# Sharing single columns between two paths, TensorE with ScalarE and VectorE, at the end of a masked reconstruction loss

## The chip, the cores and the metric

One core of a Trainium2 chip. The metric is device time in microseconds (us) of one execution. Beside it every run lists its *span*, from the first to the last recorded instruction of the program, and its mean TensorE clock. The kernel before takes 77.2 us, so 1% is 0.77 us.

## The reference, cut to what matters

```python
batch, num_patches, dim = 32, 196, 768        # 147 patches of each batch row are masked
mean = target.mean(axis=-1, keepdims=True)
var = target.var(axis=-1, keepdims=True)
target = (target - mean) / np.sqrt(var + 1e-6)
loss = np.mean((pred - target) ** 2, axis=-1)
return loss.mean(axis=-1)                      # 32 numbers
```

Two inputs of 4704 x 768 float32, 28.9 MB in all, are read once; 128 bytes are written.

## The kernel before

A batch row's 147 patches lie on four partitions, 37 on three of them and 36 on the fourth. A "column" is patch c of every partition, a tile of 128 x 768. Each column is loaded (all but the first targets cast to bfloat16 on the way), VectorE takes its statistics, ScalarE the root, VectorE the reciprocal, and GpSimd writes the normalised target `s`. Then (pred - s) is squared and summed by one of three ways:

```python
units = [((c, c + 1), 0, D, "ACT" if c < 18 else "DVE+ACT") for c in range(0, 24, 2)]
units.insert(2, ((REST,), 0, D, "ACT"))
units += [((24,), 0, D, "DVE"), ((25,), 0, D, "DVE+ACT"), ((26, 27), 0, D, "DVE+ACT")]
units += [((c,), 0, D, "ACT" if c % 2 else "DVE") for c in range(28, KM - 1)]
units += [((KM - 1,), 0, half, "ACT"), ((KM - 1,), half, D, "ACT")]
# ...
# "ACT": PE adds -s and pred in PSUM through identity matrices, ScalarE squares and sums
# "DVE+ACT": VectorE takes the difference, ScalarE squares and sums
# "DVE": VectorE does both
def difference(u, d0, w):
    z = zs[u, d0] = diffs.tile([P, 2 * D], BF16, name="zd")              # 4 buffers
    # ...
    pin(nc.vector.tensor_tensor(out=z[:, :w], in0=til[:, o:o + w], in1=s[:, so + d0:so + d0 + w],
                                op=ALU.subtract))

def square_dve(u, d0, w, dest):
    z = zs[u, d0][:, :w]
    pin(nc.vector.scalar_tensor_tensor(out=z, in0=z, scalar=1.0, in1=z, op0=ALU.mult, op1=ALU.mult,
                                       accum_out=dest))
```

KM is 36, so column 35 is the last; its pred is loaded in two halves of 384. The order of instructions on each engine is fixed when the kernel is built, by a list scheduler in the kernel that works with estimated durations and with earliest times for what has to land first. At the end small matmuls with a mask add the partial sums over partitions into `acc`; VectorE copies it and one transfer writes it.

Of the kernel before, what the change touches and what calls it, by code (L numbers as in the profile page):

```python
# [7 lines left out]
F32 = mybir.dt.float32  # L8
BF16 = mybir.dt.bfloat16
ALU = mybir.AluOpType  # L10
ACTF = mybir.ActivationFunctionType
# [3 lines left out]
def kernel(  # L15
# [7 lines left out]
    nc = tc.nc  # L23
    pin = tc.keep_in_program_order
    B, N, D = pred.shape
    eps = 1e-6
    P = 128
    J = P // B
    KJ = (N + J - 1) // J
    KM = N - (J - 1) * KJ  # L30
    assert KJ == KM + 1
    RP = B * (J - 1)
    half = D // 2
    BANK = 512
    REST = KM
# [4 lines left out]
    def rows_of(c):  # L40
        return RP if c == REST else P
# [3 lines left out]
    diffs = ctx.enter_context(tc.tile_pool(name="diffs", bufs=4))  # L45
    small = ctx.enter_context(tc.tile_pool(name="small", bufs=8))
    singles = ctx.enter_context(tc.tile_pool(name="singles", bufs=1))
    psum = ctx.enter_context(tc.tile_pool(name="psum", bufs=2, space=bass.MemoryType.PSUM))
    psum1 = ctx.enter_context(tc.tile_pool(name="psum1", bufs=1, space=bass.MemoryType.PSUM))


# [30 lines left out]
    groups += [(c, c + 1) for c in range(16, KM, 2)]  # L82


    units = [((c, c + 1), 0, D, "ACT" if c < 18 else "DVE+ACT") for c in range(0, 24, 2)]
    units.insert(2, ((REST,), 0, D, "ACT"))
    units += [((24,), 0, D, "DVE"), ((25,), 0, D, "DVE+ACT"), ((26, 27), 0, D, "DVE+ACT")]
    units += [((c,), 0, D, "ACT" if c % 2 else "DVE") for c in range(28, KM - 1)]
    units += [((KM - 1,), 0, half, "ACT"), ((KM - 1,), half, D, "ACT")]



# [3 lines left out]
    def op(name, engine, dur, needs, fn, rank=0.0, early=0.0):  # L96
        by_name[name] = len(ops)
        ops.append((name, engine, dur, needs, fn, rank, early))
# [13 lines left out]
            KIND[kind].setdefault(c, []).append((d0, d1, til, (c - c0) * w))  # L112


    land, lanes, clock = {}, {"hw": [], "hw2": [], "sw": []}, 2.9
    for i, (kind, c0, c1, d0, d1, q) in enumerate(stream):
        w = (c1 - c0) * (d1 - d0)
        clock += w * rows_of(c0) / P * 0.915 / D + (0.0 if w >= 4 * D else 0.04)
        lanes[q].append(clock + 1.1)
        for c in range(c0, c1):  # L120
            land[kind, c, d0] = clock + 1.1
        k = len(lanes[q])
        op(("load", i), {"hw": "SP", "hw2": "ACT", "sw": "POOL"}[q], 0.6, [], lambda a=stream[i]: load(*a), rank=-1.0,
           early=0.0 if k <= 8 else lanes[q][k - 9] + 0.3)

    def landed(kind, c):
        return max(t for (k, cc, d), t in land.items() if k == kind and cc == c)

    ident = singles.tile([P, P], BF16)
# [25 lines left out]
    def bn(out, parts):  # L155

        n = parts[0].shape[0]
        st = small.tile([P, len(parts), 6], F32, name="st")
        for j, x in enumerate(parts):
            pin(nc.vector.bn_stats(out=st[:n, j, :], in_=x))  # L160
        pin(nc.vector.bn_aggr(out=out, in_=st[:n, :len(parts)]))  # L161

    def stats(g, i):
        n, K = rows_of(g[0]), len(g)
        if i == 0:
            mvs[g] = small.tile([P, K, 2], F32, name="mv")
        if not norm_pix_loss:
            return
        (_, _, til, o), = tbuf[g[i]]
        bn(mvs[g][:n, i], [til[:n, o + a:o + a + half] for a in (0, half)])  # L170

    def root(g):
        n, K = rows_of(g[0]), len(g)
        r = small.tile([P, K], F32, name="r")
        nm = small.tile([P, K], F32, name="nm")
        for i, c in enumerate(g):
            rs[c] = (r[:n, i:i + 1], nm[:n, i:i + 1])
        rs[g] = r
        if not norm_pix_loss:
            pin(nc.vector.memset(r, 1.0))  # L180
            pin(nc.vector.memset(nm, 0.0))
            return
        mv = mvs[g]
        pin(nc.scalar.activation(out=r[:n], in_=mv[:n, :, 1], func=ACTF.Sqrt, bias=eps_t[:n], scale=1.0))  # L184
        pin(nc.scalar.activation(out=nm[:n], in_=mv[:n, :, 0], func=ACTF.Copy, scale=-1.0))  # L185

    def recip(g):
        n = rows_of(g[0])
        if norm_pix_loss:
            pin(nc.vector.reciprocal(out=rs[g][:n], in_=rs[g][:n]))  # L190

    for k, g in enumerate(groups):
        for i, c in enumerate(g):
            op(("bn", c), "DVE", 1.26, [], lambda g=g, i=i: stats(g, i), rank=k - 50.0, early=landed("t", c))
        op(("root", k), "ACT", 0.55, [("bn", c) for c in g], lambda g=g: root(g), rank=-1.0)
        op(("recip", k), "DVE", 0.2, [("root", k)], lambda g=g: recip(g), rank=-60.0)

# [16 lines left out]
    zs = {}  # L214
# [5 lines left out]
    def product(u, d0, w, src, so, eye, first):  # L220
        n, z = rows_of(u[0]), zs[u, d0]
        for a in range(0, w, BANK):
            b = min(w, a + BANK)
            pin(nc.tensor.matmul(z[:n, a:b], eye[:n, :n], src[:n, so + a:so + b], start=first, stop=not first))  # L224

    def sub_target(u, d0, w):
        if (u, d0) == units[-1][:2]:
            zs[u, d0] = psum1.tile([P, BANK], F32, name="z_last")
        else:
            zs[u, d0] = psum.tile([P, 3 * BANK], F32, name="z")  # L230
        s, so = sbuf[u[0]]
        product(u, d0, w, s, so + d0, nident, True)

# [15 lines left out]
    def square_dve(u, d0, w, dest):  # L249
        z = zs[u, d0][:, :w]  # L250
        pin(nc.vector.scalar_tensor_tensor(out=z, in0=z, scalar=1.0, in1=z, op0=ALU.mult, op1=ALU.mult,  # L251
                                           accum_out=dest))

    tail = 5
    n_early = len(units) - 1 - tail
    rl = singles.tile([P, n_early], F32)
    rl_sum = singles.tile([P, 1], F32)
    finals = []
    early_ops, users, seen = [], [], set()
    for k, (u, d0, d1, eng) in enumerate(units):  # L260
        w = len(u) * D if len(u) > 1 else d1 - d0
        arrive = max(t for (kk, c, d), t in land.items() if kk == "p" and c in u and d < d1)
        norms = [("norm", c) for c in u]
        for c in u:
            if c not in seen:
                op(("norm", c), "POOL", 1.02, [("recip", group_of[c])], lambda u=u, c=c: normalise(u, c), rank=k)
                seen.add(c)
        if k < len(units) - tail:
            if u[0] == REST:
                dest = singles.tile([P, 1], F32, name="rl_rest")  # L270
                finals.append((("sq", k), dest, mask_rest, RP))
            else:
                dest = rl[:, len(early_ops):len(early_ops) + 1]
                early_ops.append(("sq", k))
        else:
            dest = singles.tile([P, 1], F32, name=f"rl{k}")
            finals.append((("sq", k), dest, mask, P))
        if eng in ("DVE", "DVE+ACT"):
            op(("diff", k), "DVE", 0.57 * w / D + 0.05, norms, lambda u=u, d0=d0, w=w: difference(u, d0, w), rank=-2.0,
               early=arrive)  # L280
            if eng == "DVE":
                op(("sq", k), "DVE", 1.0 * w / D, [("diff", k)],
                   lambda u=u, d0=d0, w=w, dest=dest: square_dve(u, d0, w, dest), rank=-1.0)
            else:
                op(("sq", k), "ACT", 0.75 * w / D + 0.25, [("diff", k)],
                   lambda u=u, d0=d0, w=w, dest=dest: square_act(u, d0, w, dest), rank=k)
            continue
        op(("subt", k), "PE", 0.37 * w / D, norms + (users[-2:-1] if k < len(units) - 1 else []) + ["ident"],
           lambda u=u, d0=d0, w=w: sub_target(u, d0, w), rank=k + 0.0)
        op(("pred", k), "PE", 0.37 * w / D, [("subt", k)], lambda u=u, d0=d0, w=w: add_pred(u, d0, w), rank=k,  # L290
           early=arrive)
        op(("sq", k), "ACT", 0.73 * w / D + 0.23, [("pred", k)],
           lambda u=u, d0=d0, w=w, dest=dest: square_act(u, d0, w, dest), rank=k)
        users.append(("sq", k))

    acc = psum1.tile([1, B], F32)
    def early_sum():
        junk = singles.tile([P, n_early], F32, name="junk")
        pin(nc.scalar.activation(out=junk, in_=rl, func=ACTF.Copy, accum_out=rl_sum))

    op("rl_sum", "ACT", 0.4, early_ops, early_sum, rank=50.0)
    finals.insert(0, ("rl_sum", rl_sum, mask, P))
    turn = []

    def final(vec, m, n):
        turn.append(n)
        pin(nc.tensor.matmul(acc, vec[:n], m[:n], start=len(turn) == 1, stop=len(turn) == len(finals)))  # L307

    for i, (need, vec, m, n) in enumerate(finals):
        op(("final", i), "PE", 0.2, [need, "masks"], lambda v=vec, m=m, n=n: final(v, m, n), rank=90.0)  # L310


    HOP = 0.15
# [3 lines left out]
    while left:  # L317
        best = None
        for i in left:
            name, engine, dur, needs, fn, rank, early = ops[i]  # L320
            if any(x not in end for x in needs):
                continue
            t = max([free[engine], early] + [end[x] + (0.0 if ops[by_name[x]][1] == engine else HOP) for x in needs])
# [4 lines left out]
        _, i, t = best  # L328
        name, engine, dur, needs, fn, rank, early = ops[i]
# [43 lines left out]
```

## Time and profile before

| | kernel before |
|---|---|
| time, median of six runs | 77.22 us (77.09 to 77.56) |
| span of the profiled run (its time) | 75.4 us (77.09 us) |
| VectorE busy, instructions | 56.3 us, 148 |
| GpSimd busy | 54.4 us |
| ScalarE busy | 32.0 us |
| last half of column 35: last data record, completion | 71.20 us, 71.50 us |

No engine is busy for more than 75% of the span, but the transfers are busy from the third of forty slices to the thirty-seventh. So a change to engines can only gain at the end, after the stream. The prediction shows the lines of that end. In the profiled run 77.09 - 75.40 = 1.7 us of the time lie outside the span.

### The profile page before, as it was taken

The page shows a single profiled execution, that of the slowest core. Times are in us where ns is not written, and L with a number is a line of the kernel's source. Part 1 is how long each engine was busy: PE and PEld are TensorE (multiplying, and loading weights), DVE is VectorE, ACT ScalarE, POOL GpSimd, SP SyncE. Part 2 cuts the span into 40 slices and gives each one's busy share as a digit, 9 for nine tenths or more (in the row PEclk, how much of TensorE's full clock was granted, in tenths as well). Part 3 has the DMA queues.
Part 4 walks back from the last instruction along what each step waited for, and adds up shares of the span by engine and source line. Part 5 has one row for each costly group of instructions (what it writes and reads, how often), then busy time and mean ns, then how long its engine had stood idle before and what let it go on. Part 6 is the DMA issues. An engine that isn't in the chain of part 4 may idle for free.

```text
span 75.4 us, 570 instructions
## 1 busy us (share of the span) xinstructions
PE 30.3 (40%) x87; PEld 8.7 (11%) x88; DVE 56.3 (75%) x148; ACT 32.0 (42%) x73; POOL 54.4 (72%) x77
## 2 busy tenths in 40 slices
PE   0000000038596540688700778287544000348860
PEld 0000000001232110211100211031111000112220
DVE  0000099999999999976999928960999989989940
ACT  1400000210229802289210297239366099799550
POOL 4998205099999999499989898999878799800000
PEclk9999999999999997555555557965995555555555
DMA  0899999999999999999999999999999999999700
GB/s 0 215 424 339 262 192 236 218 209 215 212 215 215 212 216 225 212 209 215 215 212 215 219 212 225 209 212 202 214 215 209 215 210 210 214 205 205 117 0 0
DMA packets 3973, 15.41 MB, mean 204 GB/s; under 512 B 450, under 2 KB 1186, under 8 KB 3842
## 3 DMA queue, kind: packets, MB, share of 16 engines
q0 software_dynamic: 3712, 13.52, 89.2%
q1 hardware_dynamic: 146, 1.57, 5.7%
q10 hardware_dynamic: 112, 0.29, 1.0%
q14 instruction: 3, 0.02, 0.1%
HBM read 28.90 MB, written 0.00 MB: 383 GB/s over the span
## 4 chain that ended last, share of the span: by engine, by line
DMA 60%; DVE 18%; POOL 9%; issue 6%; PE 2%; ACT 1%; POOLq 0%; ACTq 0%
DMA t<-in_target_dram 49%; DVE st L160 14%; DMA p<-in_pred_dram 11%; POOL s L210 8%; DVE mv L161 3%; DVE zd L246 1%; PE acc L307 1%; POOL t L110 1%; PE z L224 1%; ACT z_last L239 1%; PE z_last L224 1%; POOLq L368 0%; DVE r L190 0%; POOL p L110 0%; DVE ob L336 0%
## 5 line engine op out<-in xcount | busy, mean ns | idle before, releaser
L160 DVE BATCH_NORM_STATS2 st<-t 128x6 f32<-128x384 bf16 (+2 forms) x74 | 36.3, 532 | 11.6 <-DMA t<-in_target_dram 11.6
L210 POOL TENSOR_SCALAR s<-t,nm,r 128x768 bf16<-128x768 bf16 (+2 forms) x37 | 38.2, 1040 | 3.2 <-ACT nm L185 2.0
L224 PE MATMUL z<-s,nident 128*128 128x512 bf16 (+4 forms) x36 | 14.6, 511 | 23.3 <-POOL s L210 17.6
L239 ACT ACTIVATE z<-z 128x1536 f32<-128x1536 f32 (+3 forms) x14 | 16.6, 1184 | 6.9 <-PE z L224 6.8
L224 PE MATMUL z<-p,ident 128*128 128x512 bf16 (+4 forms) x35 | 14.2, 542 | 12.1 <-DMA p<-in_pred_dram 12.0
L184 ACT ACTIVATE r<-mv,eps_t 128x2 f32<-128x2 f32 (+2 forms) x15 | 4.4, 293 | 29.5 <-DVE mv L161 28.8
L110 POOL DMA_DIRECT2D p<-in_pred_dram x18 | 10.2, 565 | 2.7 <-DVE st L160 1.0
L246 DVE TENSOR_TENSOR zd<-p,s 128x768 bf16<-128x768 bf16 (+1 forms) x10 | 9.7, 991 | 0.5 <-ACT zd L239 0.3
L161 DVE BATCH_NORM_AGGREGATE mv<-st 128x2 f32<-128x12 f32 (+1 forms) x37 | 7.7, 209 | 1.3
L110 POOL DMA_DIRECT2D t<-in_target_dram x8 | 4.9, 628 | 4.7 <-DMA t<-in_target_dram 3.9
L239 ACT ACTIVATE zd<-zd 128x1536 bf16<-128x1536 bf16 (+1 forms) x5 | 6.7, 1345 | 2.7 <-DVE zd L246 2.7
L224 PEld LDWEIGHTS <-ident 128*128 128x128 bf16 (+1 forms) x37 | 4.7, 126 | 27.2 <-issue 26.2
L224 PEld LDWEIGHTS <-nident 128*128 128x128 bf16 (+1 forms) x37 | 3.4, 114 | 34.6 <-issue 14.4
L251 DVE SCALAR_TENSOR_TENSOR zd<-zd 128x768 bf16<-128x768 bf16 x5 | 4.8, 955 | 0.1
L224 PE MATMUL z_last<-s,nident 128*128 128x384 bf16 x1 | 0.5, 479 | 7.1 <-POOL s L210 7.1
L190 DVE RECIPROCAL r<-r 128x2 f32<-128x2 f32 (+2 forms) x15 | 1.9, 123 | 1.7 <-ACT r L184 1.7
L185 ACT ACTIVATE nm<-mv 128x2 f32<-128x2 f32 (+2 forms) x15 | 2.8, 188 | 0.0
L239 ACT ACTIVATION_READ_ACCUMULATOR z<-z 128x1 f32 (+1 forms) x14 | 2.7, 190 | 0.0
L184 ACT ACT_TABLE_LOAD x1 | 1.3, 1283 | 1.5 <-PEq L354 1.5
L307 PE MATMUL acc<-mask,rl 128*1 128x32 f32 x10 | 1.0, 224 | 0.4 <-ACT z_last L239 0.4
L239 ACT ACTIVATION_READ_ACCUMULATOR zd<-zd 128x1 f32 x5 | 0.9, 187 | 0.0
L336 DVE COPY ob<-acc 1x32 f32<-1x32 f32 x1 | 0.2, 178 | 1.0 <-PE acc L307 1.0
(26 smaller groups left out, 5.8 us busy)
## 6 DMA issues: line engine op xcount, KB each, us to landing
t<-in_target_dram POOLq DMA_DIRECT2D x8, 768.0 KB, 24.5
p<-in_pred_dram POOLq DMA_DIRECT2D x4, 768.0 KB, 27.4
p<-in_pred_dram POOLq DMA_DIRECT2D x8, 384.0 KB, 20.9
t<-in_target_dram SPq DMA_DIRECT2D x1, 1536.0 KB, 8.4
p<-in_pred_dram POOLq DMA_DIRECT2D x3, 192.0 KB, 12.7
t<-in_target_dram ACTq DMA_DIRECT2D x1, 288.0 KB, 9.6
p<-in_pred_dram POOLq DMA_DIRECT2D x2, 96.0 KB, 7.3
p<-in_pred_dram POOLq DMA_DIRECT2D x1, 144.0 KB, 10.4
```

What stands on the lines that cost most here:

```text
L110: pin(eng.dma_start(out=til[:n], in_=src))
L160: pin(nc.vector.bn_stats(out=st[:n, j, :], in_=x))
L161: pin(nc.vector.bn_aggr(out=out, in_=st[:n, :len(parts)]))
L184: pin(nc.scalar.activation(out=r[:n], in_=mv[:n, :, 1], func=ACTF.Sqrt, bias=eps_t[:n], scale=1.0))
L185: pin(nc.scalar.activation(out=nm[:n], in_=mv[:n, :, 0], func=ACTF.Copy, scale=-1.0))
L190: pin(nc.vector.reciprocal(out=rs[g][:n], in_=rs[g][:n]))
L210: pin(nc.gpsimd.tensor_scalar(out=s[:n, so:so + D], in0=til[:n, o:o + D], scalar1=nm, scalar2=r, op0=ALU.add, op1=ALU.mult))
L224: pin(nc.tensor.matmul(z[:n, a:b], eye[:n, :n], src[:n, so + a:so + b], start=first, stop=not first))
L239: pin(nc.scalar.activation(out=z[:n, :w], in_=z[:n, :w], func=ACTF.Square, accum_out=dest[:n]))
L246: pin(nc.vector.tensor_tensor(out=z[:, :w], in0=til[:, o:o + w], in1=s[:, so + d0:so + d0 + w], op=ALU.subtract))
L251: pin(nc.vector.scalar_tensor_tensor(out=z, in0=z, scalar=1.0, in1=z, op0=ALU.mult, op1=ALU.mult, accum_out=dest))
L307: pin(nc.tensor.matmul(acc, vec[:n], m[:n], start=len(turn) == 1, stop=len(turn) == len(finals)))
```

## The change

The intent: from column 26 on, each column is worked on by both paths at once, so that neither has a whole column to do when the last one lands. PE (TensorE) and ScalarE take 512 elements (`BANK` in the kernel), VectorE takes 256. The last column is split in halves. The cut diff:

```diff
-    psum = ctx.enter_context(tc.tile_pool(name="psum", bufs=2, space=bass.MemoryType.PSUM))
-    units = [((c, c + 1), 0, D, "ACT" if c < 18 else "DVE+ACT") for c in range(0, 24, 2)]
+    units = [((c, c + 1), 0, D, "ACT" if c < 16 else "DVE+ACT") for c in range(0, 24, 2)]
-    units += [((24,), 0, D, "DVE"), ((25,), 0, D, "DVE+ACT"), ((26, 27), 0, D, "DVE+ACT")]
-    units += [((c,), 0, D, "ACT" if c % 2 else "DVE") for c in range(28, KM - 1)]
-    units += [((KM - 1,), 0, half, "ACT"), ((KM - 1,), half, D, "ACT")]
+    units += [((24,), 0, D, "DVE"), ((25,), 0, D, "DVE+ACT")]
+    for c in range(26, KM - 1):
+        units += [((c,), 0, BANK, "ACT"), ((c,), BANK, D, "DVE")]
+    units += [((KM - 1,), 0, half, "ACT"), ((KM - 1,), half, D, "DVE")]
 ...  (statistics of columns 32 and later become less urgent to the scheduler)
-            op(("bn", c), "DVE", 1.26, ..., rank=k - 50.0, early=landed("t", c))
+            op(("bn", c), "DVE", 1.26, ..., rank=k - 50.0 if c < 32 else -1.5, early=landed("t", c))
 ...  (once the pairs on PE are done, their PSUM is closed and six one-bank tiles take its place)
+                pools["stack"].close()
+                pools["parts"] = ctx.enter_context(tc.tile_pool(name="parts", bufs=6, ...PSUM))
 ...  (the early partial sums are added by VectorE, no longer by ScalarE)
-        pin(nc.scalar.activation(out=junk, in_=rl, func=ACTF.Copy, accum_out=rl_sum))
+    op("rl_sum", "DVE", 0.2, early_ops, lambda: pin(nc.vector.tensor_reduce(out=rl_sum, in_=rl, ...)))
```

The rest of the diff changes estimated durations and earliest times of the scheduler, and how many of the last pieces are summed apart from the early sum (4, before 5).

More of the change, by code (lines that the diff above doesn't have):

```diff
@@ L112, in load @@
             KIND[kind].setdefault(c, []).append((d0, d1, til, (c - c0) * w))
-    land, lanes, clock = {}, {"hw": [], "hw2": [], "sw": []}, 2.9
+    land, lanes, clock = {}, {"hw": [], "hw2": [], "sw": []}, 2.8
     for i, (kind, c0, c1, d0, d1, q) in enumerate(stream):
@@ L193 @@
         for i, c in enumerate(g):
-            op(("bn", c), "DVE", 1.26, [], lambda g=g, i=i: stats(g, i), rank=k - 50.0, early=landed("t", c))
+            op(("bn", c), "DVE", 1.26, [], lambda g=g, i=i: stats(g, i), rank=k - 50.0 if c < 32 else -1.5, early=landed("t", c))
         op(("root", k), "ACT", 0.55, [("bn", c) for c in g], lambda g=g: root(g), rank=-1.0)
@@ L226, in sub_target @@
     def sub_target(u, d0, w):
-        if (u, d0) == units[-1][:2]:
-            zs[u, d0] = psum1.tile([P, BANK], F32, name="z_last")
-        else:
-            zs[u, d0] = psum.tile([P, 3 * BANK], F32, name="z")
+        if u in pairs_pe:
+            zs[u, d0] = pools["pairs"].tile([P, 3 * BANK], F32, name="z")
+            pairs_pe.remove(u)
+        else:
+            if "parts" not in pools:
+                pools["stack"].close()
+                pools["parts"] = ctx.enter_context(tc.tile_pool(name="parts", bufs=6, space=bass.MemoryType.PSUM))
+            zs[u, d0] = pools["parts"].tile([P, BANK], F32, name="zp")
         s, so = sbuf[u[0]]
@@ L252, in square_dve @@
                                            accum_out=dest))
-    tail = 5
+    tail = 4
     n_early = len(units) - 1 - tail
@@ L257 @@
     rl_sum = singles.tile([P, 1], F32)
+    pairs_pe = [u for u, _, _, eng in units if eng == "ACT" and (len(u) == 2 or u[0] == REST)]
+    n_pairs = len(pairs_pe)
+    pools = {"stack": ExitStack()}
+    pools["pairs"] = pools["stack"].enter_context(tc.tile_pool(name="psum", bufs=2, space=bass.MemoryType.PSUM))
     finals = []
@@ L284 @@
             else:
-                op(("sq", k), "ACT", 0.75 * w / D + 0.25, [("diff", k)],
+                op(("sq", k), "ACT", 0.65 * w / D + 0.22, [("diff", k)],
                    lambda u=u, d0=d0, w=w, dest=dest: square_act(u, d0, w, dest), rank=k)
             continue
-        op(("subt", k), "PE", 0.37 * w / D, norms + (users[-2:-1] if k < len(units) - 1 else []) + ["ident"],
+        op(("subt", k), "PE", 0.37 * w / D, norms + (users[-2:-1] if len(users) < n_pairs else users[n_pairs - 1:n_pairs] + users[n_pairs:][-6:-5]) + ["ident"],
            lambda u=u, d0=d0, w=w: sub_target(u, d0, w), rank=k + 0.0)
@@ L291 @@
            early=arrive)
-        op(("sq", k), "ACT", 0.73 * w / D + 0.23, [("pred", k)],
+        op(("sq", k), "ACT", 0.65 * w / D + 0.22, [("pred", k)],
            lambda u=u, d0=d0, w=w, dest=dest: square_act(u, d0, w, dest), rank=k)
@@ L296 @@
     acc = psum1.tile([1, B], F32)
-    def early_sum():
-        junk = singles.tile([P, n_early], F32, name="junk")
-        pin(nc.scalar.activation(out=junk, in_=rl, func=ACTF.Copy, accum_out=rl_sum))
-    op("rl_sum", "ACT", 0.4, early_ops, early_sum, rank=50.0)
+    op("rl_sum", "DVE", 0.2, early_ops, lambda: pin(nc.vector.tensor_reduce(
+        out=rl_sum, in_=rl, axis=mybir.AxisListType.X, op=ALU.add)), rank=-3.0)
     finals.insert(0, ("rl_sum", rl_sum, mask, P))
@@ L309 @@
     for i, (need, vec, m, n) in enumerate(finals):
-        op(("final", i), "PE", 0.2, [need, "masks"], lambda v=vec, m=m, n=n: final(v, m, n), rank=90.0)
+        op(("final", i), "PE", 0.2, [need, "masks"], lambda v=vec, m=m, n=n: final(v, m, n), rank=90.0,
+           early=max(land.values()) + 0.4)
     HOP = 0.15
```

## The prediction

> **What bounds the kernel now.** I read the page first, then the windows, then the chain of work that ended last, then the timeline of the last 20 us.
>
> The page's slices say that the transfers are busy from the third slice to the thirty-seventh, and the windows put an edge to it (columns: stretch, length, busy time of PE, PEld, DVE, ACT and POOL, clock of PE, DMA share, GB/s written):
>
> ```profile
> DMA  0899999999999999999999999999999999999700
> ...
> HBM read 28.90 MB, written 0.00 MB: 383 GB/s over the span
> ```
>
> ```profile
> 20.00:40.00 20.00, 11.22 (x32) 3.29 (x31) 18.44 (x56) 9.00 (x23) 18.38 (x22) 0.73 1.04 215
> ...
> 70.00:71.00 1.00, 0.79 (x4) 0.19 (x3) 1.00 (x3) 0.37 (x1) 0.00 (x0) 0.50 1.11 166
> 71.00:72.00 1.00, 0.95 (x6) 0.28 (x5) 0.97 (x2) 0.97 (x4) 0.00 (x0) 0.50 0.03 4
> ```
>
> The reader is to see a stream that never pauses and then stops at 71.0 us. Nearly all of it is float32 in memory and bfloat16 in the chip, so 215 GB/s written is some 430 GB/s read. The diff changes no transfer, so 71.0 us is a floor for the arrival of the last column. After it comes a tail of 75.4 - 71.0 = 4.4 us, and the chain shows what that tail is:
>
> ```profile
> 62.66 8.34 DMA p<-in_pred_dram
> 71.00 0.04 issue
> 71.05 0.48 PE z L224
> 71.53 0.33 PE acc L307 x4
> 71.85 0.45 PE z_last L224
> 72.30 0.02 issue
> 72.32 0.47 ACT z_last L239
> 72.80 0.12 ACTq L368
> 72.91 0.04 issue
> 72.96 0.28 PE acc L307 x2
> 73.23 0.02 issue
> 73.26 0.18 DVE ob L336
> ```
>
> PE adds the two halves of column 35 one after the other with sums between, ScalarE squares the second at 72.32, the sum over partitions starts at 72.96, the copy ends at 73.44, and writing the result takes the remaining 1.95 us. So 1.91 us lie between the last byte (71.05) and the last sum (72.96). That, and nothing else, is open to this change.
>
> VectorE is the second thing to look at. It works without a pause worth naming from 57.45 to 72.26, and part of that is not work but waiting on GpSimd:
>
> ```profile
> 57.38 1.94 POOL L210 TENSOR_SCALAR s<-t,nm,r 128x768 bf16<-128x768 bf16 x2
> 57.45 2.69 DVE L246 TENSOR_TENSOR zd<-p,s 128x1536 bf16<-128x1536 bf16 x1
> ...
> 60.13 1.80 DVE L246 TENSOR_TENSOR zd<-p,s 128x1536 bf16<-128x1536 bf16 x2
> ...
> 60.42 2.29 POOL L210 TENSOR_SCALAR s<-t,nm,r 128x768 bf16<-128x768 bf16 x1 [0.59 <-DVE r L190]
> ```
>
> One difference of two columns takes 0.9 us when two run in 1.80, but 2.69 us when two normalisations of GpSimd began just before it. And one normalisation, 0.97 us alone, took 2.29 behind two such differences.
>
> [...]57.45 + 2.69 = 60.14 is the end of the two normalisations (59.32) plus 0.82 us.[...]
>
> **The change part by part.** (1) Columns 16 and 17 move from PE to a VectorE difference; columns 26 and 27 leave it. So there are four differences of 1536 on VectorE as before. (2) Before, the single columns 24, 28, 30, 32, 34 were VectorE's whole (difference and square), and 29, 31, 33, 35 PE's and ScalarE's. Now each of 26 to 34 gives 256 of its 768 elements to VectorE. Elements of these nine columns on VectorE's two-input instructions: before 4 x 768 differenced and squared, plus 1536 differenced; after 9 x 256 = 2304 of each. (3) The last column is split in halves that run on both paths at once. (4) Columns 34 and 35 get their statistics later, between the differences. (5) PSUM is regrouped into six one-bank parts, so matmuls of s for six columns can be done early. (6) The early sum goes from ScalarE (0.22 + 0.19 us) to one small VectorE reduce.
>
> The durations, with the rows they come from:
>
> ```profile
> L246 DVE TENSOR_TENSOR zd<-p,s 128x768 bf16<-128x768 bf16 x6 | 3.6, 617 | 0.5 <-ACT zd L239 0.3 <-DMA p<-in_pred_dram 0.2
> L251 DVE SCALAR_TENSOR_TENSOR zd<-zd 128x768 bf16<-128x768 bf16 x5 | 4.8, 955 | 0.1
> ...
> L239 ACT ACTIVATE z<-z 128x768 f32<-128x768 f32 x3 | 2.4, 793 | 0.9 <-PE z L224 0.9
> ...
> L239 ACT ACTIVATE z<-z 128x384 f32<-128x384 f32 x1 | 0.5, 475 | 0.0
> ```
>
> From starts in the timeline: a 768 square occupies VectorE 0.88 us (69.83 to 70.71), and a 768 difference 0.59 when the next instruction needs it, about 0.47 when not. Differences of 1536 repeat every 0.87 to 0.9, so 768 elements cost 0.4 us[...]. Fixed parts: [...]0.07 for a difference, 0.19 when waited for. Estimates from these: [...]difference of 256 0.20, or 0.32 when waited for; of 384 0.39. ScalarE, between 475 ns for 384 and 793 for 768, takes about 0.58 for 512.
>
> VectorE's sum from the first difference on: before, 4 x 0.9 + 6 x 0.56 + 5 x 0.88 = 11.4 us, spread over 14.8[...]. After: 4 x 0.9 + 2 x 0.5 + 0.88 + nine columns (six at 0.55, three at 0.67) 5.3 + last half 0.87 + reduce 0.15 = 11.8 us, plus statistics of two columns (2 x 1.13) that used to stand before. So the change doesn't lighten VectorE. It gains by smaller pieces at the very end.
>
> Laying it out with the landings of before (columns 24/25 at 62.2, 26/27 about 64.0, 28/29 65.8, 30/31 67.7, then 68.6, 69.5, 70.5, 71.0): differences of 16 and 18 from 55.1, ending about 57.4. Statistics of 34 lie beside the normalisations of 32 and 33 (57.4 to 59.3), where before a difference stood blocked. Differences of 20 and 22 to 61.1, statistics of 35 to 62.3, differences of 24 and 25 to 63.2. Normalisations of 34 and 35 then run 63.4 to 65.3: the first lies in VectorE's wait for columns 26/27, the second holds it up by about 1 us. From 65.35: two differences 0.4, squares 0.88 + 0.35, two differences 0.4, three squares 1.05, two differences 0.4, two squares 0.7 gives 69.55; columns 32, 33, 34 at 0.67 each, 71.55; reduce 71.7; last half 0.39 + 0.48 + 0.08, ending at 72.65. The other path: column 35's first half 71.05, matmul 0.48, square and read 0.66 after column 34's square, about 72.3. The last sum thus starts at 72.7 against 72.96: a gain of 0.25 us.
>
> With both engines idle at the landing, the last half would take 71.05 + 0.95 = 72.0, and the gain would be 0.95 us. That is the most this tail can give, 1.2%.
>
> **The rivals.** *VectorE becomes the end.* From column 26 on, twenty small instructions stand where nine large ones stood. If each costs 0.05 us more than estimated, the end moves by 1.0 us and the kernel is 0.75 us slower, about 78.0. For it speaks that my layout leaves VectorE no wait after 65.3; against, that the page's fixed parts are measured. [...]Two normalisations at 63.4 to 65.3 could instead alternate with the small instructions; the stolen time is about the same 1 us either way, but if column 35's normalisation starves behind VectorE, both paths of the last column wait; it has 5 us of slack, so I think it hidden. *VectorE catches up by 71.* If my small costs are too high by 0.03 us, the whole 0.95 us is won, 76.3.[...]
>
> **Range and chances.** The layout says 77.2 - 0.25 = 76.95; the catching-up rival says 76.3 and the small-instruction rival 78.0. I lean a little to the gain, since the earlier differences are blocked less, and put 76.85, with 76.2 to 77.6. Over 2% faster needs 1.54 us, more than the 0.95 us that the floor leaves: 0.02. Over 2% slower needs 1.8 us more work on VectorE than laid out: 0.03.
>
> **What would show it.** The transfers should still stop at 71.0; if not, the floor is wrong. The last square on VectorE should start near 72.1 and last 0.5; the 256-element square should show a spacing near 0.35 and the difference 0.2 to 0.3. The chain should end through VectorE, not ScalarE; if ScalarE's last square ends later, the order of the two paths is wrong. Normalisations of 34 and 35 should lie near 63.4 to 65.3.

Its sum came to a last sum at 72.7 us against 72.96, a gain of 0.25 us, so 76.95 us, and 76.85 was put. Two of its terms, 0.35 us for a square of 256 and 0.48 for one of 384, stay in the layout as estimates, as does 0.15 for the reduce. Of the "fixed parts" called measured, only those of a difference are. The changed kernel's trace later shows 0.35, 0.48 (72.06 to 72.54) and 0.18 for the three.

## The result

| | before | changed |
|---|---|---|
| time, median of six runs | 77.22 us (77.09 to 77.56) | 77.26 us (77.13 to 77.36) |
| ratio | | 1.0002, 95% interval 0.9979 to 1.0025 |
| span of the profiled run | 75.4 us | 75.1 us |
| VectorE instructions | 148 | 167 |

A ratio is the mean time of one kernel's fast runs over that of the other's of the same rounds, so it isn't quite the ratio of the medians.

The time is the same, though the span of the profile is 0.3 us shorter. First the end of the chain of the changed kernel (start, length, what), which answers to the chain shown in the prediction:

```profile
62.44 9.13 DMA p<-in_pred_dram
71.57 0.03 issue
...
71.67 0.37 DVE zd L251
...
72.06 0.58 DVE zd L256 x2
...
72.68 0.28 PE acc L313 x2
...
72.98 0.18 DVE ob L344
```

The chain now runs through VectorE. The last sum starts at 72.68, where it was 72.96, and the copy ends at 73.16, where it was 73.44. But the transfer in it ends at 71.57. The windows over the same time say that almost no bytes moved by then:

```profile
70.00:71.00 1.00, 0.43 (x2) 0.10 (x1) 0.94 (x6) 1.00 (x4) 0.00 (x0) 1.00 1.05 158
71.00:72.00 1.00, 0.73 (x9) 0.29 (x8) 0.86 (x4) 0.94 (x4) 0.00 (x0) 1.00 0.04 6
```

The two views do not contradict each other. In the trace the last data record of the stream ends at 71.29, and the last of the sixteen semaphore updates that complete the last piece comes at 71.57. The first half of column 35 completes at 71.08. In the kernel before the same three times are 71.20, 71.50 and 71.00. There the late completion does not show in the chain, because PE came to the second half only at 71.78.

Next the instructions of the changed kernel near the end, from the timeline (start, length, engine, line, operation, tiles, count):

```profile
63.74 2.87 POOL L210 TENSOR_SCALAR s<-t,nm,r 128x768 bf16<-128x768 bf16 x2 [0.77 <-DVE r L190]
...
64.11 0.94 DVE L251 TENSOR_TENSOR zd<-p,s 128x256 bf16<-128x256 bf16 x2 [0.58 <-DMA p<-in_pred_dram]
...
65.85 1.03 DVE L256 SCALAR_TENSOR_TENSOR zd<-zd 128x256 bf16<-128x256 bf16 x1
...
67.56 0.41 DVE L256 SCALAR_TENSOR_TENSOR zd<-zd 128x256 bf16<-128x256 bf16 x1
...
67.91 0.41 DVE L256 SCALAR_TENSOR_TENSOR zd<-zd 128x256 bf16<-128x256 bf16 x1
...
69.35 0.28 DVE L251 TENSOR_TENSOR zd<-p,s 128x256 bf16<-128x256 bf16 x1
...
69.67 0.42 DVE L256 SCALAR_TENSOR_TENSOR zd<-zd 128x256 bf16<-128x256 bf16 x1
...
71.36 0.18 DVE L306 TENSOR_REDUCE rl_sum<-rl 128x1 f32<-128x30 f32 x1
```

A square of 256 repeats after 0.35 us (67.56 to 67.91). A difference that its square waits for starts at 69.35 and the square at 69.67, 0.32 later. The normalisations of columns 34 and 35 hold VectorE up twice: two differences took 0.94 in place of 0.4, and a square of 256 took 1.03 in place of 0.41. That is about 1.2 us. VectorE has done its reduction at 71.54, and the last half lands at 71.57: it arrives just in time.

So inside the program nearly all went as laid out. The missing 0.3 us are outside it: 77.20 - 75.12 = 2.08 us in this profiled run, against 1.70 before. What lies there the page does not show, but the trace has the records of semaphores. After the span of the kernel before, updates of one semaphore follow in steps, then five groups of 47 to 51 semaphores are updated, then a second round of steps ends 1.90 us after the span. In the changed kernel these records agree to 0.01 us up to the fifth step, 0.54 us after the span. The sixth comes at 1.01, where it came at 0.63 before, and all that follows is as late, but for the first group. From the sixth step on something makes the closing of the program 0.38 us late.

### The profile page after: what moved, and what is told of

Its sections match the earlier page's. It is cut to its first block, busy times and chain, and to the rows that moved or that the text cites. A ratio compares the mean times of both kernels' runs of the same rounds, so it can differ in the third digit from the quotient of the medians.

```text
span 75.1 us, 595 instructions
## 1 busy us (share of the span) xinstructions
PE 29.9 (40%) x83; PEld 8.9 (12%) x84; DVE 56.1 (75%) x167; ACT 32.6 (43%) x79; POOL 53.0 (71%) x77
## 4 chain that ended last, share of the span: by engine, by line
DMA 52%; DVE 23%; POOL 16%; issue 6%; PE 0%; POOLq 0%; DVEq 0%
DMA p<-in_pred_dram 41%; DVE st L160 17%; POOL s L210 13%; DMA t<-in_target_dram 11%; DVE mv L161 4%; POOL p L110 2%; DVE zd L256 1%; DVE zd L251 0%; PE acc L313 0%; DVE ob L344 0%; DVE r L190 0%; POOLq L210 0%; DVEq L251 0%
## 5 line engine op out<-in xcount | busy, mean ns | idle before, releaser
L210 POOL TENSOR_SCALAR s<-t,nm,r 128x768 bf16<-128x768 bf16 (+2 forms) x37 | 36.8, 1001 | 3.5 <-ACT nm L185 2.0
L224 PE MATMUL z<-s,nident 128*128 128x512 bf16 (+2 forms) x26 | 10.5, 512 | 23.4 <-POOL s L210 20.1
L244 ACT ACTIVATE z<-z 128x1536 f32<-128x1536 f32 (+1 forms) x9 | 12.3, 1363 | 10.3 <-PE z L224 10.3
L224 PE MATMUL z<-p,ident 128*128 128x512 bf16 (+2 forms) x25 | 11.2, 604 | 7.3 <-DMA p<-in_pred_dram 7.1
L251 DVE TENSOR_TENSOR zd<-p,s 128x256 bf16<-128x256 bf16 (+3 forms) x16 | 8.9, 575 | 0.9 <-DMA p<-in_pred_dram 0.6
L224 PE MATMUL zp<-p,ident 128*128 128x512 bf16 (+1 forms) x10 | 4.5, 511 | 9.3 <-DMA p<-in_pred_dram 9.1
L244 ACT ACTIVATE zp<-zp 128x512 f32<-128x512 f32 (+1 forms) x10 | 5.7, 573 | 0.7 <-PE zp L224 0.6
L256 DVE SCALAR_TENSOR_TENSOR zd<-zd 128x256 bf16<-128x256 bf16 (+2 forms) x11 | 5.6, 534 | 0.1
L224 PE MATMUL zp<-s,nident 128*128 128x512 bf16 (+1 forms) x10 | 3.8, 482 | 2.5 <-ACT z L244 2.1
L244 ACT ACTIVATION_READ_ACCUMULATOR zp<-zp 128x1 f32 x10 | 1.9, 188 | 0.0
```

The costliest lines, as they stand in the source:

```text
L210: pin(nc.gpsimd.tensor_scalar(out=s[:n, so:so + D], in0=til[:n, o:o + D], scalar1=nm, scalar2=r, op0=ALU.add, op1=ALU.mult))
L224: pin(nc.tensor.matmul(z[:n, a:b], eye[:n, :n], src[:n, so + a:so + b], start=first, stop=not first))
L244: pin(nc.scalar.activation(out=z[:n, :w], in_=z[:n, :w], func=ACTF.Square, accum_out=dest[:n]))
```

## The experiments

Twelve kernels ran, on two chips, with the kernel before in the same rounds. "Outside" is time minus span, the mean over a kernel's fast runs. The first row is the kernel before beside the first four experiments.

| kernel | VectorE instr. | span, mean | outside, mean | ratio to before, 95% interval |
|---|---|---|---|---|
| before, same rounds | 148 | 75.40 | 1.71 | |
| before again | 148 | 75.42 | 1.70 | 1.0001 (0.9988 to 1.0013) |
| changed again | 167 | 75.00 | 2.11 | 1.0000 (0.9987 to 1.0012) |
| before + 26 memsets | 174 | 75.47 | 1.71 | 1.0008 (0.9995 to 1.0022) |
| changed, column 24's square to ScalarE | 165 | 75.18 | 1.92 | 0.9999 (0.9963 to 1.0035) |
| changed + 7 memsets | 174 | 74.97 | 1.70 | 0.9942 (0.9927 to 0.9956) |
| before + 19 memsets | 167 | 75.40 | 2.04 | 1.0043 (1.0030 to 1.0056) |
| before, split of the last column alone | 151 | 75.88 | 1.73 | 1.0064 (1.0051 to 1.0077) |
| changed, without that split | 164 | 75.38 | 1.71 | 0.9997 (0.9983 to 1.0010) |
| changed + 2 memsets (second chip) | 169 | 75.13 | 1.85 | 0.9974 (0.9958 to 0.9990) |
| changed + 7 on ScalarE (second chip) | 167 | 75.06 | 2.09 | 0.9995 (0.9980 to 1.0011) |
| changed + 7 memsets, last column 512 to 256 (second chip) | 174 | 75.10 | 1.71 | 0.9952 (0.9933 to 0.9970) |
| changed, statistics early (second chip) | 167 | 75.77 | 1.94 | 1.0064 (1.0049 to 1.0080) |

On the second chip the kernel before had a mean span of 75.48 and 1.71 outside.

### Is the time outside the span a property of the kernel?

The edit of the first two: none. Each is the kernel as it stands.

> The kernel before, unchanged, run as an experiment so that every one of its runs shows a span beside its time. The one profile of before had span 75.4 us at time 77.09, so 1.7 us lay outside the span; the changed kernel has 75.1 to 75.3 at 77.13 to 77.36, so 2.1 us outside. Theory A (the change lengthens what lies outside the span): spans here about 75.4 to 75.6 and 1.7 us outside in every run. Theory B (the one profile of before was an odd run): about 2.1 us outside, with spans of 75.1 to 75.2, no different from the changed kernel's, and then the 0.28 us that the two profiles differ by is only one run's scatter.

> The changed kernel, unchanged, on the same chip: ratio 0.999 to 1.002 by both theories; 2.05 us outside the span. It gives a tighter interval than the six runs had.

Theory A held: the change lengthens what lies outside the span. Six runs of the kernel before had 1.66 to 1.73 us outside their spans, and the eleven runs beside them 1.68 to 1.77. Six runs of the changed kernel had 2.09 to 2.13. So the change does shorten the span, by 0.40 us in the mean (75.40 to 75.00), and does lengthen what lies outside it, by 0.40 us (1.71 to 2.11). The two cancel.

What makes the closing longer? A first guess was the bare number of instructions:

```diff
-    op("eps", "DVE", 0.1, [], lambda: pin(nc.vector.memset(eps_t, eps)))
+    pad_t = singles.tile([P, 1], F32, name="pad_t")
+    def pads():
+        pin(nc.vector.memset(eps_t, eps))
+        for _ in range(26):
+            pin(nc.vector.memset(pad_t, 0.0))
+    op("eps", "DVE", 0.1, [], pads)
```

> The kernel before with 26 one-element memsets on VectorE before the first data arrive, where it idles, so that it has as many instructions more as the changed kernel has. Theory A with the number of instructions as its cause: span as before (75.4), time longer by about 0.4 us, 77.6. Theory B, or A with another cause: time as before within 0.1 us.

No: 26 more instructions than before, more than the changed kernel has, and still 1.71 us outside. That theory A with the count as its cause fell.

### Which stream, and how sharp?

The trace has one more hint: records of instruction fetches, 8,192 bytes each, on a queue of their own. In the profiled run of the kernel before there are three within the span and none after it. In the changed kernel there are three, and a fourth 1.6 us after the span; in the padded kernel a fourth 1.3 us after it. The first of them moves with VectorE's count: it comes at 27.7 us in both kernels, and at 18.9 with the 26 memsets, and in all three VectorE had begun 53 or 54 recorded instructions one microsecond earlier. That suggests a theory C, the author's guess from these records: the place in VectorE's stream where the next fetch falls decides whether the program waits for it at its end. The memsets above shift that place and do no work, since VectorE waits for data until 9.1 us (9.11 in the padded kernel). With 7 memsets in the changed kernel, and 19 in the kernel before:

> The changed kernel with seven one-element memsets on VectorE in its idle time before the first data. In the runs so far the time minus the span is 1.7 us with 148 and with 174 VectorE instructions (kernel before, and padded) and 2.0 to 2.1 us with 167 and 165 (changed kernel, light)[...]. Theory C (where the VectorE instruction stream ends against its fetches decides it): with 174 instructions the span stays 75.0 and 1.7 us lie outside, time 76.7, ratio 0.995. Theory D (the changed kernel's closing is longer for another reason, its pools or its size): 2.07 us outside, time 77.1, ratio 1.000.

> The kernel before with 19 such memsets, so that VectorE has 167 instructions as in the changed kernel. Theory C: span 75.3 as before, 2.07 us outside, time 77.4, ratio 1.005. Theory D: 1.7 us outside, time 77.05, ratio 1.000 as the padded one with 26.

The times that theory C forecast came on both sides. Seven instructions *more* make the changed kernel 0.44 us faster than without them (76.67 against 77.11 in the mean), with the same span; nineteen make the kernel before 0.32 us slower (77.44 against 77.12), with the same span. The profile of the changed kernel with seven memsets shows the fourth fetch inside the span, where the unpadded one showed three (queue, packets, MB, share):

```profile
q14 instruction: 4, 0.03, 0.1%
```

Its fourth fetch is at 72.73, before the end of the program, and its closing records have the times of the kernel before. The trace of the other side does not fit so well: the kernel before with nineteen memsets has no fetch after its span, and its closing records end at 1.90 us as without them. Its added 0.33 us outside the span (2.04 against 1.71) show in none of these records.

Two more on the second chip ask how sharp this is and whether another engine would do. The first has `range(2)` in place of `range(7)`. The second puts the padding on ScalarE:

```diff
+    def act_pads():
+        for _ in range(7):
+            pin(nc.scalar.activation(out=pad_t, in_=eps_t, func=ACTF.Copy, scale=-1.0))
+    op("act_pads", "ACT", 1.4, ["eps"], act_pads, rank=-70.0)
```

> The changed kernel with two one-element memsets on VectorE in place of the seven. VectorE's stream has 191 records then, one more than the padded kernel before (190, 1.7 us outside the span), where the changed kernel has 189 and 2.07 us. If the place of one instruction fetch in VectorE's stream decides it: 1.7 us outside, time 76.7, ratio 0.995. If seven instructions helped in another way: 2.07 us, ratio 1.000.

> The control: the changed kernel with seven tiny activations[...] on ScalarE in its idle time at the start instead of memsets on VectorE. If it is VectorE's stream: no help, span 75.0, 2.07 us outside, ratio 1.000. If any longer program helps, or ScalarE's stream matters: 1.7 us outside, ratio 0.995.

Two instructions give back two thirds of it: 1.85 us outside. Here it is the fourth step of the closing that comes late, by 0.13 us, and the rest with it. Neither expectation, all of it or nothing, was right. Seven activations more on ScalarE give nothing: 2.09. So here it is VectorE's stream that decides, and in the changed kernel a shift of seven instructions removes the delay.

What stays open is what the closing waits for. The runs show that shifting its stream moves the delay or removes it; that a fetch is the cause is argued from its place and not shown, and the traces speak against the simplest form of it. In the changed kernel the fetch after the span starts at 1.61 us, 0.60 after the late step at 1.01. The kernel before with 26 memsets has such a fetch (1.32 us) and no delay; with nineteen it has a delay and no such fetch.

The traces do show that the pause sits at different places of the closing. In the kernels with column 24's square on ScalarE and with the early statistics told of below (1.92 and 1.94 us outside) every step is on time, and one group of 51 updates alone begins at 1.14 and 1.15 us where it begins at 0.77 in the kernel before: 0.37 late, as the sixth step is in the changed kernel (0.38). Nor does the count of instructions order the kernels. The one without the split of the last column has 164 and no delay (1.71), while its neighbour with 165 has 1.92 and the kernel before with 167 has 2.04. What orders them these records do not show.

### What sets the end inside the span?

The prediction laid VectorE's backlog as the limit of the last half. Take 0.88 us of it away:

```diff
-    units += [((24,), 0, D, "DVE"), ((25,), 0, D, "DVE+ACT")]
+    units += [((24,), 0, D, "DVE+ACT"), ((25,), 0, D, "DVE+ACT")]
-                op(("sq", k), "ACT", 0.65 * w / D + 0.22, [("diff", k)],
+                op(("sq", k), "ACT", 0.0 if u == (24,) else 0.65 * w / D + 0.22, [("diff", k)],
```

(The second edit only keeps the scheduler's order as it was.)

> The changed kernel with the square of column 24 (0.88 us of VectorE) given to ScalarE; the order is else the same. If VectorE's backlog is what sets the end (it started the last half at 71.67, 0.6 us after the half had landed at about 71.05), VectorE's last square now ends about 72.05 and ScalarE's first half of column 35 at 72.3 sets the last sum: the last sum starts at 72.35 instead of 72.68, 0.3 us less span. If the end is held by something else (landing of the last half later than 71.05), the last sum stays at 72.6 to 72.7.

The lighter VectorE did not bring the last half forward. From its timeline:

```profile
71.37 0.18 DVE L306 TENSOR_REDUCE rl_sum<-rl 128x1 f32<-128x30 f32 x1
...
71.59 0.36 DVE L251 TENSOR_TENSOR zd<-p,s 128x384 bf16<-128x384 bf16 x1
```

The last half completes at 71.49 in that trace and its difference starts 0.09 later, as it does in the unaltered one (71.57 and 71.67; 0.09 before rounding). VectorE's reduction before it doesn't set the start: it ends 0.06 after the landing in the one (71.55) and 0.03 before it in the other (71.54). In all seven kept traces of the changed kernel and its variants in which the statistics stay late and VectorE takes the last piece, the start follows the completion by 0.09. So the rival expectation was right: what holds the end is the completion of the last half, and the backlog is gone about by then. The mean span was no better than the changed kernel's, 75.18 with one run at 75.9 in it, 75.04 without that one.

Now the split of the last column, alone and left out:

```diff
 (on the kernel before)
-    units += [((KM - 1,), 0, half, "ACT"), ((KM - 1,), half, D, "ACT")]
+    units += [((KM - 1,), 0, half, "ACT"), ((KM - 1,), half, D, "DVE")]
 (on the changed kernel, the reverse)
```

> The kernel before with one part of the change alone: the second half of the last column goes to VectorE. The last half lands at 71.5 in both traces. VectorE's order then has its difference before the square of column 34 (0.96 us), so it starts at 71.5, the square of 34 runs 71.9 to 72.75, the last square to 73.3: last sum at 73.35 instead of 72.95, span 75.7, 1.7 us outside (151 VectorE instructions), time 77.45, ratio 1.005. If the split of the last column is a gain by itself: last sum before 72.9.

> The changed kernel without the split of the last column: both halves of column 35 by PE and ScalarE. Second half landed 71.5, matmul to 72.0, square 72.2 to 72.8 after the first half's: last sum at 72.9, span 75.3, so the split is worth 0.3 us of span to the changed kernel; with 164 VectorE instructions 2.0 us outside by theory C, time 77.3, ratio 1.003. If VectorE was the limit of the changed kernel, the last sum comes earlier than 72.6 instead.

Alone, the split costs 0.47 us of span, because VectorE then still owes column 34's square:

```profile
71.71 0.36 DVE L246 TENSOR_TENSOR zd<-p,s 128x384 bf16<-128x384 bf16 x1 [0.35 <-ACT z L239]
71.99 0.95 DVE L251 SCALAR_TENSOR_TENSOR zd<-zd 128x768 bf16<-128x768 bf16 x1
...
72.86 0.55 DVE L251 SCALAR_TENSOR_TENSOR zd<-zd 128x384 bf16<-128x384 bf16 x1
```

A whole square of 768 stands between the last half's difference and its square. Left out of the changed kernel, it costs 0.38 us of span (75.38 against 75.00), which is all that the change gains there. The rest of the change, the sharing of columns 26 to 34 among it, gains nothing by itself; it clears VectorE so that the split pays. Both expectations of span held within 0.2 us. The second's time did not: 77.07, where 77.3 was expected with a late closing.

If the completion of the last piece is the limit, a smaller last piece should help:

```diff
-    piece("p", KM - 1, KM, 0, half)
-    piece("p", KM - 1, KM, half, D)
+    piece("p", KM - 1, KM, 0, BANK)
+    piece("p", KM - 1, KM, BANK, D)
-    units += [((KM - 1,), 0, half, "ACT"), ((KM - 1,), half, D, "DVE")]
+    units += [((KM - 1,), 0, BANK, "ACT"), ((KM - 1,), BANK, D, "DVE")]
```

> The changed kernel with seven memsets and the last column split 512 to 256 instead of 384 to 384, in its two transfers too. The last piece still completes at 71.5, but VectorE needs 0.32 and 0.43 us for it instead of 0.40 and 0.56: ready at 72.25. ScalarE's 512 lands about 71.17, matmul 0.45, square 0.58 and read 0.1 after column 34's: 72.35. If the landing of the last piece is the bound: last sum at 72.4 instead of 72.6, span 74.8, time 76.5, ratio 0.992. If VectorE's or ScalarE's backlog is the bound: no change from the kernel with seven memsets, 0.994.

A miss. The 512 landed near the 71.17 expected (their matmul starts at 71.26) and their matmul took 0.38, not 0.45. VectorE finished the smaller piece at 72.41, 0.2 us earlier than the 72.62 of the changed kernel, but the chain moved to ScalarE:

```profile
71.17 0.51 ACT zp L251 x2
...
72.44 0.13 ACT zp L251
...
72.61 0.29 PE acc L320 x4
```

ScalarE squares the 512 of column 34 from 71.26 to 71.85 and those of column 35 after it, ready at 72.56. So the halves were balanced: with 384 to 384 VectorE ends at 72.62 and ScalarE at 72.28, with 512 to 256 it is 72.41 and 72.56.

### The order of the statistics

```diff
-            ... rank=k - 50.0 if c < 32 else -1.5, early=landed("t", c))
+            ... rank=k - 50.0, early=landed("t", c))
```

This also lets column 36's statistics come early, as they did before the change.

> The changed kernel with its fourth part undone: statistics of columns 34 and 35 before the first differences, at the old rank (column 36's come early again too). Prediction's view[...]: VectorE still arrives at the last half by about 71.6 and the span is 75.0 to 75.3. Rival (normalisations beside differences cost VectorE over 0.5 us more than beside statistics): VectorE arrives 0.5 to 1 us late, last sum at 73.2 or later, span over 75.5.

Here my view fell and the rival held: 0.29 us more span than the kernel before of the same rounds, and 0.64 more than the changed kernel with two memsets on that chip (75.77 against 75.13). The timeline of the early order, VectorE and GpSimd:

```profile
57.57 1.94 POOL L210 TENSOR_SCALAR s<-t,nm,r 128x768 bf16<-128x768 bf16 x2
57.63 2.68 DVE L251 TENSOR_TENSOR zd<-p,s 128x1536 bf16<-128x1536 bf16 x1
...
60.32 4.23 DVE L251 TENSOR_TENSOR zd<-p,s 128x1536 bf16<-128x1536 bf16 x5
60.60 3.07 POOL L210 TENSOR_SCALAR s<-t,nm,r 128x768 bf16<-128x768 bf16 x1 [0.59 <-DVE r L190]
...
66.42 0.29 DVE L251 TENSOR_TENSOR zd<-p,s 128x256 bf16<-128x256 bf16 x1 [0.89 <-ACT zd L244]
```

The first difference is blocked until 60.3, as in the kernel before. ScalarE therefore starts its squares late (at 60.35, where the changed kernel's first began at 56.55), gives the four difference buffers back late, and VectorE stands idle 0.89 us for one of them at 66.4. It comes to the last half at 72.41, 0.72 after it has landed (71.69). In the changed kernel the statistics of column 34 lie beside the normalisations of 32 and 33, and two differences come before them. At 0.64 us of span it is worth more than the split of the last column.

## Why the prediction was right or wrong

**The floor: right in its substance, wrong by 0.5 us in its place.** The stream is unchanged, its last completion 71.50 before and 71.57 after. But I took the last half as landed at 71.05. The 71.00 in the chain is the completion of the first half. That of the second comes at 71.50 in the kernel before and 71.57 in the changed one. So "1.91 us lie between the last byte (71.05) and the last sum" was really 1.46 us between the landing and the last sum, and "the gain would be 0.95 us" as an upper end was really about 0.5: 71.5 + 0.95 = 72.45 against 72.96. In both traces the completion comes 0.28 to 0.30 us after the last data record.

**The layout of VectorE: right.** Square of 256: 0.35 estimated, 0.35 measured (with 0.88 for 768, 1.04 ns for each further element). Difference waited for: 0.32 and 0.32. Last half: 0.39 to the square's start and 0.56 for the square, 0.39 and 0.56 measured, with its read. The normalisations took about 1.2 us from VectorE where about 1 us was laid. The last sum was put at 72.7 and came at 72.68. One thing was luck: I had VectorE's backlog end at 71.7 as the limit, where it ended at 71.54 and the landing at 71.57 was the limit; both give the same end. And the gain was laid to smaller pieces at the very end alone, with only a lean for the later statistics; the runs give those 0.64 us of span, without which the change would have lost.

**The rivals.** The small instructions did not cost more, so VectorE did not become the end. VectorE caught up, but that won no 0.95 us, since the landing was later than I had it. PE, a rival, did not bind; in the profiled run its clock from 70 to 72 us was 1.00 and not the 0.50 of the kernel before, and its matmul of 384 for the last column's first half took 0.32 us where it took 0.48 before. The remark that the stolen time "is about the same 1 us either way" was made of how the normalisations of columns 34 and 35 lie among the small instructions, and that was not tested. Taken more widely, that stolen time costs the same wherever it falls, it is refuted by the early statistics, which I had not listed as a rival: there the stolen time reaches ScalarE and comes back as a wait for buffers.

**From span to time: the step that failed.** "The layout says 77.2 - 0.25 = 76.95" assumes that all that follows the last sum takes as long as before, in the prediction's words "writing the result takes the remaining 1.95 us", and that what lies outside the span stays the same. The first holds: 75.4 - 73.44 = 1.96 before, 75.12 - 73.16 = 1.96 after. The second doesn't: 1.71 became 2.11 us. That 0.40 us is the term of the sum that was left out, and it takes back the whole gain of the span, 0.40 us in the mean. The mechanism inside the program was right, and its size about so: 0.25 us laid out, 0.28 at the last sum in the two profiles, 0.40 of span in the mean. With seven idle memsets, which take the added term away, the changed kernel runs in 76.68 us, against the 76.85 predicted. What the closing waits for stays open.

**What the forecast was worth.** The lean to a gain was not borne out in the time: 77.26 us against 77.22.

## What to carry to other kernels

When a span and a time disagree, list time minus span for every run of both kernels before looking for a cause inside the program; here it told a 0.4 us gain and a 0.4 us loss apart in which the ratio saw nothing. Seven idle instructions in one engine's stream were worth 0.44 us here, as much as the redesigned tail, so compare variants of a tuned kernel with their streams shifted by a handful of instructions before keeping or dropping one. And take a landing from the completion that the waiting engine sees, not from where the bytes stop.
